# The S5 output maps of a hybrid decoder layer, made one step earlier in a generator

## The chip, the cores and the metric

The kernel runs on one core of a Trainium2 chip. The metric is the device time of one execution in microseconds; a time is the median of several executions. The core's engines are named as the profile names them: PE (matrix products; PEld are its weight loads), DVE (vector), ACT (scalar and activation functions), POOL (a second, general vector engine), SP (which here issues most DMAs). Each engine works through its own list of instructions in order and waits on semaphores for the others. SBUF is the on-chip memory that all engines read. PSUM is the accumulator memory that PE writes, divided here into eight banks of 512 float32 numbers per partition.

## The reference, cut to what matters

One decoder layer on a (1, 1024, 1024) float32 stream: a normalised input `h` is projected once by `w_in`, and the projection feeds three branches (an S5 state-space model, a Mamba-2 block and a cross-attention), which gates merge; then follow an output projection, a gated feed-forward block and a final norm. The change lies in the S5 branch:

```python
def s5_mixer(u, lam_re, lam_im, log_dt, b_re, b_im, c_re, c_im, d):
    ...
    bu_re = jnp.einsum('blgk,gpk->blgp', ug, bbr)
    bu_im = jnp.einsum('blgk,gpk->blgp', ug, bbi)
    ...
    _, _, xr, xi = lax.associative_scan(combine, (a_re, a_im, bu_re, bu_im), axis=1)
    y = jnp.einsum('gkp,blgp->blgk', c_re, xr) - jnp.einsum('gkp,blgp->blgk', c_im, xi)
    return y.reshape(bsz, L, D_S5) + d * u
```

There are 64 groups of 16 channels with 64 complex states each, over 1024 time steps.

## The kernel before, in words

**The stage.** The kernel computes the S5 recurrence in blocks of 8 time steps. The 64 groups are taken in four quarters (`q` = 0 to 3) of 16 groups. For one quarter it needs:

- *input maps* `BA` (`b_maps`, line 830): the matrices that carry 8 steps of input into one state, as products of `b` with powers of the state's multiplier. DVE makes them in six operations of 128x1024, all from SBUF to SBUF (`cmap`, line 816: four products, then a subtraction and an addition). PE transposes them in four blocks of four 128x128 pieces, each block into a PSUM bank `s5bps`, and ACT copies the blocks out as `s5BTr` and `s5BTi` (`b_transpose`, line 857).
- *output maps* `CA`: PE transposes the raw `c` into a PSUM bank `s5cps` (`c_transpose`, line 841, two matrix products); ACT copies that bank to the first step of `s5CAr` and `s5CAi`, and DVE makes the other eight steps with the same `cmap`, whose four products read `s5cps` from PSUM and whose last two operations read SBUF alone (`c_maps`, line 848).
- *lag matrices* (`lag_maps`, line 869): PE multiplies `CA` with `bd`, a block-diagonal copy of the input maps, into `s5kps` (16 pairs, `s5CAr` and `s5CAi` in turn). ACT copies the result, DVE adds the diagonal `s5dg`, and DMAs take it through the buffer `kS` in DRAM into `s5T`.
- *phases* `R`: POOL doubles the vectors `s5Rr` and `s5Ri` seven times (`double`, line 900).
- *sums, scan, back*: PE makes `s5sr` and `s5si` from the input and `BT`; DVE rotates them by `R`, scans, and rotates back into `s5Hr` and `s5Hi`.
- *outputs and gelu*, for the quarter before: PE makes `s5yp` from `s5T`, `s5Hr`, `s5Hi` and `CA`, in two halves `y0` and `y1`; ACT and DVE apply GELU to each half in turn (`gelu`, line 983), and DMAs store it.

**What runs beside it.** `s5_work` (line 778) is a generator. Between its `yield`s PE runs the matrix products of the projection: 4 query tiles `qt` and 9 gate tiles `gt`, each in two halves of 24 products 128x512 into a PSUM bank `gh`. After each 12 of them `tick` (line 329) is called, and lets the generator go on when its credit is positive; the numbers in `S5_LAG` (line 189) say how many ticks lie after each step. The weights of these tiles come by DMA into `wr`, and ACT and DVE split each into a high and a low part, `wh` and `wl`.

**What sets the order.** In this stage the order on PE, ACT and SP is that of the program text (`TE.on = SY.on = S.on = True`, line 1155). DVE and POOL are ordered by the scheduler of the tile framework, which also decides, by its own forecast of when buffers come free, which of the six small PSUM banks (pool `ps`) a tile gets. PE's waits follow from that choice.

**The names in the trace.** All instructions go through one helper, so that they all have line 51, and the tiles tell them apart. PE's products with 128x512 are written `gh<-hlH,wh` and so on.

Of the kernel before, what the change touches and what calls it, by code (L numbers as in the profile page):

```python
# [58 lines left out]
def hybrid_layer(ctx: ExitStack, tc: tile.TileContext, a: dict, out: bass.AP):  # L59
# [77 lines left out]
    def copy(o, i, scale=1.0):  # L137
        S.activation(out=o, in_=i, func=AF.Copy, scale=scale)
# [639 lines left out]
    def s5_work():  # L778

        with ExitStack() as es:  # L780
# [16 lines left out]
            def fl(t, s0, n):  # L797
                return t.rearrange("p j s k -> p j (s k)")[:, :, s0 * 16:(s0 + n) * 16]
# [17 lines left out]
            def cmap(o, s0, wr, wi, p2, jj):  # L816

                shp = [P, 8, 8, 16]
                orr, oi = (t[:, :, s0:s0 + 8, :] for t in o)
                w = [x.unsqueeze(2).to_broadcast(shp) for x in (wr, wi)]  # L820
                p_ = [bc(x[:, jj, :], 16) for x in p2]
                t1, t2 = (wt().rearrange("p j (t k) -> p j t k", t=8) for _ in range(2))
                tt(orr, w[0], p_[0], ALU.mult)
                tt(t1, w[1], p_[1], ALU.mult)
                tt(oi, w[0], p_[1], ALU.mult)
                tt(t2, w[1], p_[0], ALU.mult)
                tt(orr, orr, t1, ALU.subtract)
                tt(oi, oi, t2, ALU.add)

            def b_maps(jj, braw):  # L830

                BAr = sp.tile([P, 8, 8, 16], F32, tag="BAr", name="s5BAr")
                BAi = sp.tile([P, 8, 8, 16], F32, tag="BAi", name="s5BAi")
                cmap((BAr, BAi), 0, braw[:, 0], braw[:, 1], (pfr, pfi), jj)
                for g2 in range(2):
                    pp = slice(g2 * 64, (g2 + 1) * 64)
                    V.tensor_copy(bd[pp, 0, :, g2, :], BAr[pp, :, 7, :])
                    ts(bd[pp, 1, :, g2, :], BAi[pp, :, 7, :], -1.0, ALU.mult)
                return BAr, BAi

            def c_transpose(craw):
                cps = ps.tile([P, 2, 8, 16], F32, tag="s", name="s5cps")
                for ri in range(2):
                    TE.transpose(cps[:, ri].rearrange("p j k -> p (j k)"),
                                 craw[:, ri].rearrange("p g c -> p (g c)"), ident)
                return cps

            def c_maps(jj, cps):

                CAr = sp.tile([P, 8, 9, 16], F32, tag="CAr", name="s5CAr")  # L850
                CAi = sp.tile([P, 8, 9, 16], F32, tag="CAi", name="s5CAi")
                copy(CAr[:, :, 0, :], cps[:, 0])
                copy(CAi[:, :, 0, :], cps[:, 1])
                cmap((CAr, CAi), 1, cps[:, 0], cps[:, 1], (pwr, pwi), jj)
                return CAr, CAi
# [12 lines left out]

            def lag_maps(q, CA):

                ksq = kS[q % 2]
                ktw = wt()
                for hh in range(2):
                    kps = ps.tile([32, 4, P], F32, tag="s", name="s5kps")
                    for j in range(4):
                        jx = hh * 4 + j
                        for ri in range(2):
                            TE.matmul(kps[:, j, :], bd[:, ri, jx].rearrange("p g k -> p (g k)"),
                                      fl(CA[ri], 0, 8)[:, jx, :], start=ri == 0, stop=ri == 1)
                    KT = ktw[0:32, 4 * hh:4 * hh + 4, :]  # L880
                    copy(KT, kps)
                    dg = sp.tile([32, 4, 16], F32, tag="dg", name="s5dg")
                    tt(dg, bc(dk[:, 8 * q + 4 * hh:8 * q + 4 * hh + 4], 16),
                       id16.unsqueeze(1).to_broadcast([32, 4, 16]), ALU.mult)
                    tt(KT[:, :, 0:16], KT[:, :, 0:16], dg, ALU.add)
                    SY.dma_start(out=ksq[4 * hh:4 * hh + 4].rearrange("j p x -> p j x"), in_=KT)
                kv_ = ksq.rearrange("j (g k) x -> k j g x", g=2)
                for s in range(8):
                    tz = Tz[s * 16:(s + 1) * 16].rearrange("p (j g) t k -> p j g (t k)", g=2)
                    SY.dma_start(out=tz[:, :, :, s * 16:P], in_=kv_[:, :, :, 0:P - s * 16])  # L890

            def phases(jj):

                Rr = sp.tile([P, 8, P], F32, tag="Rr", name="s5Rr")
                Ri = sp.tile([P, 8, P], F32, tag="Ri", name="s5Ri")
                G.memset(Rr[:, :, 0:1], 1.0)
                G.memset(Ri[:, :, 0:1], 0.0)
                return Rr, Ri

            def double(R, jj, ks):  # L900
                Rr, Ri = R
                for k in ks:
                    n = 1 << k
                    tmp = sp.tile([P, 8, 64], F32, tag="ph", name="s5ph")[:, :, 0:n]
                    e_r, e_i = bc(er[:, k, jj], n), bc(ei[:, k, jj], n)
                    r0, i0, r1, i1 = Rr[:, :, 0:n], Ri[:, :, 0:n], Rr[:, :, n:2 * n], Ri[:, :, n:2 * n]
                    tt(r1, e_r, r0, ALU.mult, G)
                    tt(tmp, e_i, i0, ALU.mult, G)
                    tt(r1, r1, tmp, ALU.subtract, G)
                    tt(i1, e_r, i0, ALU.mult, G)  # L910
                    tt(tmp, e_i, r0, ALU.mult, G)
                    tt(i1, i1, tmp, ALU.add, G)
# [53 lines left out]

            def outputs(hh, U, CA):

                yps = [ps.tile([P, 4, P], F32, tag="s", name="s5yp") for _ in range(2)]
                for j in range(4):  # L970
                    jx = hh * 4 + j
                    for g2 in range(2):
                        g = 2 * jx + g2
                        TE.matmul(yps[g2][:, j, :], Tz[:, g].rearrange("p t k -> p (t k)"), U[:, g, :],
                                  start=True, stop=False)
                    for cm, hm, last in ((CA[0], Hr, False), (CA[1], Hi, True)):
                        for g2 in range(2):
                            pp = slice(g2 * 64, (g2 + 1) * 64)
                            TE.matmul(yps[g2][:, j, :], fl(cm, 1, 8)[pp, jx, :], hm[pp, jx, :],
                                      start=False, stop=last)  # L980
                return yps
# [23 lines left out]
            for q in range(5):  # L1005
                jj = slice(8 * q, 8 * q + 8)
                if old:
                    qo, Uo, CAo = old
                    y0 = outputs(0, Uo, CAo)
                if q < 4:  # L1010
                    U, braw, craw = nl
                    BA = b_maps(jj, braw)
                    R = phases(jj)
                    double(R, jj, range(5))
                yield S5_LAG[0]
                if old:
                    y1 = outputs(1, Uo, CAo)
                    Y0 = gelu(qo, 0, y0)
                if q < 4:
                    cps = c_transpose(craw)  # L1020
                    double(R, jj, [5])
                yield S5_LAG[1]
                if q < 4:
                    BT = b_transpose(BA)
                    double(R, jj, [6])
                    CA = c_maps(jj, cps)
                if old:
                    y_store(qo, 0, Y0)
                    Y1 = gelu(qo, 1, y1)
                yield S5_LAG[2]  # L1030
                if q == 4:
                    s5_end.append(lambda: y_store(qo, 1, Y1))
                    break
                lag_maps(q, CA)
                if old:
                    y_store(qo, 1, Y1)
                if q < 3:
                    nl = loads(q + 1)
                yield S5_LAG[3]
                D0 = decay(jj)  # L1040
                s0 = sums(0, BT, U)
                s1 = sums(1, BT, U)
                yield S5_LAG[4]
                W = [sp.tile([P, 8, P], F32, tag=t_, name="s5W") for t_ in ("BAr", "BAi")]
                scan(0, s0, R, D0, W)
                back(0, R, W)
                scan(1, s1, R, D0, W)
                yield S5_LAG[5]
                back(1, R, W)
                old = q, U, CA  # L1050

# [102 lines left out]
    set_banks("2", 1, 6, True)  # L1154
    TE.on = SY.on = S.on = True
    s5 = s5_work()
    next(s5)
    a1_epi(*a1_last[0])
# [298 lines left out]
    for m in G_SSD:  # L1457
        if m == G_SSD[-1]:
# [3 lines left out]
            cps = ExitStack()  # L1462
# [415 lines left out]
```

## Time and profile before

| | |
|---|---|
| time, median of 3 executions | 2279.96 us (2277.62 to 2281.93) |
| the profiled execution, its time | 2283.63 us |
| the profiled execution, its span (first to last instruction) | 2281.9 us |
| PE busy | 2212.3 us, 97% of the span |
| DVE busy | 1614.5 us, 71% |
| ACT busy | 988.3 us, 43% |
| POOL busy | 791.3 us, 35% |
| the stretch 515 to 754 us, in which the S5 stage lies | PE busy 225.88 of 239.00 us, DVE 186.48, ACT 65.58, POOL 118.38 |
| the stretch 754 to 906 us (attention) | PE busy 149.17 of 152.00 us |
| the stretch 1115 to 1532 us (merge) | PE busy 404.53 of 417.00 us |

A row of a timeline names the start, the duration, the engine and the operation, what it writes and reads, the sizes, and how many like it are merged; in brackets stands how long the engine had been idle before it, and what ended that. Matrix products are pipelined: the rows of PE overlap, and the distance between starts tells the rate. A row of waits says who waited for whom, microseconds in total, how often, and the longest. A row of windows gives a stretch, its length, the busy time of PE, PEld, DVE, ACT and POOL with their instruction counts, then the granted share of the PE clock, the share of the DMA engines and GB/s.

### The profile page before, as it was taken

The page shows a single profiled execution, that of the slowest core. Times are in us where ns is not written, and L with a number is a line of the kernel's source. Part 1 is how long each engine was busy: PE and PEld are TensorE (multiplying, and loading weights), DVE is VectorE, ACT ScalarE, POOL GpSimd, SP SyncE. Part 2 cuts the span into 40 slices and gives each one's busy share as a digit, 9 for nine tenths or more (in the row PEclk, how much of TensorE's full clock was granted, in tenths as well). Part 3 has the DMA queues.
Part 4 walks back from the last instruction along what each step waited for, and adds up shares of the span by engine and source line. Part 5 has one row for each costly group of instructions (what it writes and reads, how often), then busy time and mean ns, then how long its engine had stood idle before and what let it go on. Part 6 is the DMA issues. An engine that isn't in the chain of part 4 may idle for free. (4 is left out here: it accounts for less than half of the span.)

```text
span 2281.9 us, 31065 instructions
## 1 busy us (share of the span) xinstructions
PE 2212.3 (97%) x11243; PEld 1831.3 (80%) x11243; DVE 1614.5 (71%) x2354; ACT 988.3 (43%) x1750; POOL 791.3 (35%) x605
## 2 busy tenths in 40 slices
PE   7999899999999999999989999999999999999998
PEld 6887778887777887777768878889988888888886
DVE  7779966769777576989464445542898888886665
ACT  4555354552222466666242131222345555545544
POOL 2523333326554006888156512210023343320110
PEclk9999999999999999999999999999999999999999
DMA  4333233446454438888777664523323333339654
GB/s 142 120 109 105 84 111 111 148 134 138 78 114 100 142 117 268 300 293 270 248 248 233 219 216 128 166 67 119 111 79 102 106 101 108 99 102 330 220 184 163
DMA packets 380189, 355.53 MB, mean 156 GB/s; under 512 B 35586, under 2 KB 323202, under 8 KB 380036
## 3 DMA queue, kind: packets, MB, share of 16 engines
q1 hardware_dynamic: 378880, 349.36, 49.3%
q10 hardware_dynamic: 1156, 4.20, 0.5%
q8 instruction: 88, 1.44, 0.3%
q14 instruction: 65, 0.53, 0.1%
HBM read 255.45 MB, written 98.04 MB: 155 GB/s over the span
## 5 line engine op out<-in xcount | busy, mean ns | idle before, releaser
L51 DVE TENSOR_TENSOR wl<-wr,wh 128x512 fp32r<-128x512 f32 x301 | 257.5, 865 | 195.7 <-ACT wh L51 177.6
L51 ACT ACTIVATE wh<-wr 128x512 fp32r<-128x512 f32 (+1 forms) x305 | 186.7, 625 | 348.4 <-PE g L51 149.4
L51 POOL TENSOR_TENSOR wS<-wr 128x512 f32<-128x512 f32 x82 | 144.8, 1766 | 527.9 <-DMA wr<-in_w_up 330.5
L51 PE MATMUL g<-hlL,wh 128*128 128x512 f32 x736 | 290.0, 394 | 5.3 <-DVE hlL L51 5.3
L51 PE MATMUL g<-hlH,wh 128*128 128x512 f32 x736 | 288.8, 393 | 5.5 <-ACT hlH L51 4.4
L51 PE MATMUL g<-hlH,wl 128*128 128x512 f32 x736 | 288.0, 392 | 0.0
L51 PE MATMUL gh<-hlH,wh 128*128 128x512 f32 (+1 forms) x464 | 191.4, 413 | 0.0
L51 PE MATMUL gh<-hlH,wl 128*128 128x512 f32 (+1 forms) x464 | 181.4, 391 | 0.0
L51 PE MATMUL gh<-hlL,wh 128*128 128x512 f32 (+1 forms) x464 | 181.0, 390 | 0.0
L51 DVE TENSOR_TENSOR wl<-wS,wh 128x512 fp32r<-128x512 f32 x164 | 126.8, 778 | 65.9 <-ACT wh L51 65.9
L51 PEld LDWEIGHTS g<-hlL,wh 128*128 128x128 f32 x736 | 139.0, 189 | 38.8 <-DVE hlL L51 10.8
L51 PEld LDWEIGHTS g<-hlH,wh 128*128 128x128 f32 x736 | 139.0, 189 | 35.9 <-ACT hlH L51 5.7
L51 PEld LDWEIGHTS g<-hlH,wl 128*128 128x128 f32 x736 | 139.1, 189 | 28.4
L51 ACT ACTIVATE wh<-wS 128x512 fp32r<-128x512 f32 x164 | 102.9, 628 | 127.3 <-PE wA L51 69.3
L51 POOL TENSOR_TENSOR wS<-wr,wS 128x512 f32<-128x512 f32 x41 | 93.9, 2289 | 121.0 <-DVE wl L51 119.7
L51 PE MATMUL dP<-wl,ah 128*128 128x512 f32 x308 | 120.1, 390 | 0.4 <-DVE wl L51 0.4
L51 PE MATMUL dP<-wh,ah 128*128 128x512 f32 x308 | 120.0, 389 | 0.1
L51 PE MATMUL dP<-wh,al 128*128 128x512 f32 x308 | 119.8, 389 | 0.0
L51 PEld LDWEIGHTS gh<-hlH,wh 128*128 128x128 f32 (+1 forms) x464 | 85.9, 185 | 23.9 <-issue 5.6
L51 DVE TENSOR_TENSOR al<-ra,ah 128x512 fp32r<-128x512 f32 x77 | 56.2, 730 | 67.0 <-ACT ah L51 66.9
L51 PEld LDWEIGHTS gh<-hlL,wh 128*128 128x128 f32 (+1 forms) x464 | 86.0, 185 | 21.5 <-issue 3.6
L51 PEld LDWEIGHTS gh<-hlH,wl 128*128 128x128 f32 (+1 forms) x464 | 85.8, 185 | 20.3
(382 smaller groups left out, 5822.7 us busy)
## 6 DMA issues: line engine op xcount, KB each, us to landing
wr<-in_w_in SPq DMA_DIRECT2D x76, 512.0 KB, 3.7
wr<-in_w_up SPq DMA_DIRECT2D x44, 512.0 KB, 3.7
xc<-xcS SPq DMA_DIRECT2D x32, 640.0 KB, 6.0
ra<-aS SPq DMA_DIRECT2D x77, 256.0 KB, 5.0
seg<-aD SPq DMA_DIRECT2D x32, 512.0 KB, 7.4
gi<-gS SPq DMA_DIRECT2D x32, 512.0 KB, 5.1
xcS<-xv SPq DMA_DIRECT2D x24, 512.0 KB, 2.9
gS<-gt SPq DMA_DIRECT2D x24, 512.0 KB, 3.8
```

Of the source, the lines that this page charges most:

```text
L51: r = f(*args, **kw)
```

## The change

The call of `c_maps` moves from behind `b_transpose`, one `yield` later, to directly behind `c_transpose`.

```diff
@@ -1017,13 +1017,12 @@
                     y1 = outputs(1, Uo, CAo)
                     Y0 = gelu(qo, 0, y0)
                 if q < 4:
-                    cps = c_transpose(craw)
+                    CA = c_maps(jj, c_transpose(craw))
                     double(R, jj, [5])
                 yield S5_LAG[1]
                 if q < 4:
                     BT = b_transpose(BA)
                     double(R, jj, [6])
-                    CA = c_maps(jj, cps)
                 if old:
                     y_store(qo, 0, Y0)
                     Y1 = gelu(qo, 1, y1)
```

No instruction is added or dropped. The order on SP, on POOL and of PE's matrix products stays as it was; what moves stands on ACT, on DVE in quarter 0 alone, and in the PSUM banks, and so in PE's waits.

ACT, quarter 1 (`s5Y` is the GELU of half `y0`, `qt<-gh` copies out a query tile, `s5BTr` and `s5BTi` copy out the four transposed blocks of the input maps; the words in brackets are the counters that a row waits for):

```order
 L51 ACTIVATE s5Y<-s5yp 128x4x128 [waits PE_49]
 L51 ACTIVATE s5Y<-s5Y 128x4x128 [waits DVE_49]
-L51 ACTIVATE qt<-gh 128x512 [waits PE_49,Activation_49,Pool_49]
+L51 ACTIVATE s5CAr<-s5cps 128x8x16 [waits PE_49]
+L51 ACTIVATE s5CAi<-s5cps 128x8x16
+L51 ACTIVATE qt<-gh 128x512 [waits Activation_49,Pool_49]
 L51 ACTIVATE s5BTr<-s5bps 128x512 [waits PE_49] x2
 L51 ACTIVATE s5BTi<-s5bps 128x512 [waits PE_49] x2
-L51 ACTIVATE s5CAr<-s5cps 128x8x16
-L51 ACTIVATE s5CAi<-s5cps 128x8x16
```

The two copies out of `s5cps` now stand ahead of the four copies of `s5bps`, and ahead of the copy of a projection tile. In the other quarters it is the same, but in quarter 0 they stand behind `qt<-gh`.

PE, quarter 1, the third and fourth block of the transposition of the input maps:

```order
 L51 MATMUL s5bps<-ident,s5BAi 128x128 [waits DVE_49,PE_49]
 L51 MATMUL s5bps<-ident,s5BAi 128x128 x3
-L51 MATMUL s5bps<-ident,s5BAi 128x128 [waits Activation_49]
+L51 MATMUL s5bps<-ident,s5BAi 128x128 [waits DVE_49,PE_49,Activation_49]
 L51 MATMUL s5bps<-ident,s5BAi 128x128 x3
```

The fourth block used to take the bank of the first one, once ACT had copied that out. Now it takes the bank of `s5cps`, and its first product waits for the fourth DVE product of the output maps, the last reader of that bank. Quarter 3 has the same new wait; in quarter 2 the fourth block keeps the bank of the first and its wait for ACT, and in quarter 0 it has no wait.

DVE, quarter 0, from the block-diagonal copies `s5bd` to the output maps:

```order
 L51 COPY s5bd<-s5BAr 64x8x16
 L51 TENSOR_SCALAR s5bd<-s5BAi 64x8x16
-L51 TENSOR_TENSOR s5dg<-s5dk,id_395 32x64
 L51 TENSOR_TENSOR s5CAr<-s5cps,s5pwr 128x8x128
 L51 TENSOR_TENSOR s5w<-s5cps,s5pwi 128x1024
```

The small diagonal `s5dg` goes from ahead of the output maps to behind them and the two `wl` that follow them. In quarters 1 to 3 DVE's order is unchanged: the output maps already stood directly behind the GELU of half `y0`.

## The prediction

> **What bounds the kernel now.** PE does: it is busy for 97% of the span. So I read first what PE waits for in the S5 stretch (waits, 515 to 760 us: who waited for whom, microseconds in total, times, longest).
>
> ```profile
> DVE s5CAr L51 <- ACT s5CAi L51: 18.3, 4, 7.0
> ...
> PE s5kps L51 <- DVE s5CAr L51: 6.9, 4, 1.9
> PE s5kps L51 <- DVE s5CAi L51: 6.2, 4, 1.8
> ```
>
> PE has no other wait there: 13.1 us in eight pieces, all at the lag matrices `s5kps`, all for DVE's last two operations of the output maps. DVE in turn had been idle for 18.3 us ahead of those maps, waiting for ACT's copy `s5CAi`. The timelines of the three engines in quarter 1 show why.
>
> ```profile
> 579.80 0.44 PE L51 MATMUL s5cps<-ident,s5bc 128*128 128x128 f32 x2
> 585.56 1.03 PE L51 MATMUL s5bps<-ident,s5BAr 128*128 128x128 f32 x8
> 586.43 1.07 PE L51 MATMUL s5bps<-ident,s5BAi 128*128 128x128 f32 x8
> 594.61 0.38 PE L51 MATMUL s5kps<-s5CAr,s5bd 128*32 128x128 f32 x2 [1.64 <-DVE s5CAr L51]
> 596.59 0.38 PE L51 MATMUL s5kps<-s5CAi,s5bd 128*32 128x128 f32 x2 [1.60 <-DVE s5CAi L51]
> ...
> 580.33 0.63 ACT L51 ACTIVATE s5Y<-s5Y 128x512 f32<-128x512 f32 x1 [0.86 <-DVE s5Y L51]
> ...
> 586.20 1.09 ACT L51 ACTIVATE s5BTr<-s5bps 128x512 f32<-128x512 f32 x2 [4.75 <-PE s5bps L51]
> ...
> 588.28 0.32 ACT L51 ACTIVATE s5CAi<-s5cps 128x128 f32<-128x128 f32 x1
> ...
> 581.00 0.69 DVE L51 SCALAR_TENSOR_TENSOR s5Y<-s5Y,s5yp 128x512 f32<-128x512 f32 x1 [0.70 <-ACT s5Y L51]
> 588.63 1.23 DVE L51 TENSOR_TENSOR s5CAr<-s5cps,s5pwr 128x1024 f32<-128x1024 f32 x1 [6.95 <-ACT s5CAi L51]
> ...
> 592.04 1.21 DVE L51 TENSOR_TENSOR s5w<-s5cps,s5pwr 128x1024 f32<-128x1024 f32 x1
> ...
> 594.38 2.06 DVE L51 TENSOR_TENSOR s5CAi<-s5CAi,s5w 128x1024 f32<-128x1024 f32 x1
> ```
>
> PE has transposed `c` by 580.24, but ACT copies it at 588.28, behind the copies of `s5bps`, which PE makes only at 585.56. DVE, free at 581.69, starts 6.95 us later and ends at 596.44; PE, ready for `s5kps` at 592.97 (594.61 less 1.64), stalls.
>
> The stall costs more than its length. The windows (length, busy of PE, PEld, DVE, ACT, POOL, then the granted PE clock) show PE at half clock behind it, in all four quarters:
>
> ```profile
> 539.00:543.00 4.00, 4.00 (x24) 3.43 (x23) 2.85 (x3) 0.59 (x1) 3.92 (x4) 0.57 0.13 25
> 597.00:600.50 3.50, 3.50 (x19) 2.85 (x18) 2.01 (x4) 2.56 (x5) 0.62 (x2) 0.51 0.02 5
> 600.50:604.00 3.50, 3.50 (x55) 3.29 (x55) 2.46 (x7) 3.18 (x6) 0.00 (x0) 1.00 0.56 171
> 651.50:655.00 3.50, 3.50 (x19) 2.92 (x20) 2.11 (x4) 2.22 (x5) 3.27 (x4) 0.53 0.00 0
> 710.00:713.00 3.00, 3.00 (x16) 2.49 (x15) 1.61 (x4) 1.96 (x4) 1.78 (x3) 0.50 0.00 0
> ```
>
> Length times the missing share is 1.72, 1.72, 1.65 and 1.50 us; I take 1.7 each, 6.8 in all.
>
> **The change part by part.** Nothing is added or removed; ACT's two copies and DVE's six operations start earlier. The sum is made in the profiled execution (2283.63 us, span 2281.9).
>
> *Quarter 0.* Here DVE has little idle time to give:
>
> ```profile
> 529.40 0.22 DVE L51 TENSOR_SCALAR s5bd<-s5BAi 64x128 f32<-64x128 f32 x1
> 529.63 0.21 DVE L51 TENSOR_TENSOR s5dg<-s5dk,id 32x64 f32<-32x64 f32 x1
> 531.01 1.22 DVE L51 TENSOR_TENSOR s5CAr<-s5cps,s5pwr 128x1024 f32<-128x1024 f32 x1 [1.17 <-ACT s5CAi L51]
> ...
> 537.25 0.38 PE L51 MATMUL s5kps<-s5CAr,s5bd 128*32 128x128 f32 x2 [1.81 <-DVE s5CAr L51]
> 538.80 0.38 PE L51 MATMUL s5kps<-s5CAi,s5bd 128*32 128x128 f32 x2 [1.17 <-DVE s5CAi L51]
> ...
> 545.57 1.29 POOL L51 TENSOR_TENSOR s5Ri<-s5Ri,s5ph 128x512 f32<-128x512 f32 x1
> ...
> 548.85 0.69 DVE L51 TENSOR_TENSOR s5w<-s5si,s5Ri 128x512 f32<-128x512 f32 x1 [0.17 <-PE s5si L51]
> ```
>
> The maps start at 529.62, when `s5bd` is done, not 531.01: 1.39 us earlier. Of PE's 2.98 us, 1.59 remain. Does the clock still drop? Two other gaps bound that:
>
> ```profile
> 812.00:816.00 4.00, 3.32 (x16) 2.72 (x17) 3.70 (x11) 3.29 (x11) 0.00 (x0) 1.00 0.08 30
> 1334.50:1337.50 3.00, 3.00 (x11) 2.46 (x10) 2.42 (x6) 0.00 (x0) 0.00 (x0) 0.50 0.44 131
> ...
> 812.68 0.59 PE L51 MATMUL ptps<-ident,pr 128*128 128x128 f32 x2 [2.12 <-DVE pr L51]
> ...
> 1333.12 0.60 PE L51 MATMUL ib<-dgi,ones 128*128 128x128 f32 x3 [1.86 <-DVE dgi L51]
> ```
>
> A gap of 2.12 us kept the full clock, one of 1.86 lost it; 1.59, in two pieces, lies below both, so I take no drop and keep 1.7 us for the range. Quarter 0 gains 1.39 + 1.7 = 3.1. The moved `s5dg` (0.21 us) falls into DVE's wait for `s5kps` and costs nothing, at most 0.2.
>
> *Quarter 1.* From `s5kps` on, DVE's scan follows PE's sums, so DVE moves with PE, with one exception: POOL's phases end at 546.86 whatever PE does, and DVE needs them at 548.85. DVE can come at most 1.9 us earlier while PE comes 3.1. The maps then start at 581.69 - 1.9 = 579.8, right behind `s5Y`, and their fourth product ends 4.62 us later (588.63 to 593.25), at 584.4. The maps are whole 3.2 us after that (593.25 to 596.44), at 587.6, and PE reaches `s5kps` at 589.9 at the earliest: the wait of 3.24 us and its half clock go. The new wait takes some back: the fourth transposed block stood at 586.87 (586.43 and four steps of 0.11) and is due at 586.87 - 3.1 = 583.8, 0.65 us before its bank is free. Behind it in PE's list stand the projection products of two ticks and then `s5kps`, and for the block itself wait ACT's last copy to `s5BTi` and, queued behind that on ACT, the GELU of half `y1`; all of these have the 5 us and more until `s5kps`, so the price is PE's own 0.65. Net 3.24 + 1.7 - 0.65 = 4.3. Lower bound of the new wait: 0, if POOL doesn't hold DVE back; upper: 1.2 more if DVE gains nothing in quarter 0.
>
> *Quarter 2* has no new wait at the fourth block.
>
> ```profile
> 638.08 0.69 DVE L51 SCALAR_TENSOR_TENSOR s5Y<-s5Y,s5yp 128x512 f32<-128x512 f32 x1 [0.70 <-ACT s5Y L51]
> ...
> 649.45 0.38 PE L51 MATMUL s5kps<-s5CAr,s5bd 128*32 128x128 f32 x2 [1.59 <-DVE s5CAr L51]
> ```
>
> DVE is free at 638.77; with the 7.8 us that the six operations took in quarter 1 (588.63 to 596.44) the maps are whole at 646.6, and PE comes to `s5kps` at 647.86. That is enough by 1.3 us, the smallest margin of the three. The old wait is 13.1 less the 2.98, 3.24 and 3.71 of the others, so 3.2 with rounding, and 1.7 of clock: 4.9.
>
> *Quarter 3:*
>
> ```profile
> 695.12 0.69 DVE L51 SCALAR_TENSOR_TENSOR s5Y<-s5Y,s5yp 128x512 f32<-128x512 f32 x1 [0.70 <-ACT s5Y L51]
> ...
> 699.07 1.07 PE L51 MATMUL s5bps<-ident,s5BAi 128*128 128x128 f32 x8
> 707.49 0.38 PE L51 MATMUL s5kps<-s5CAr,s5bd 128*32 128x128 f32 x2 [1.88 <-DVE s5CAr L51]
> 709.69 0.58 PE L51 MATMUL s5kps<-s5CAi,s5bd 128*32 128x128 f32 x2 [1.83 <-DVE s5CAi L51]
> ```
>
> DVE starts the maps at 695.81, their fourth product ends at 700.43, and the fourth block stood at 699.51: PE waits 0.9. Gain 3.71 + 1.7 - 0.9 = 4.5.
>
> ACT's copies (0.3 us each) take ACT's idle time, 4.75 us in quarter 1; what they delay is one copy of a projection tile, whose bank PE needs ticks later: 0, at most 0.3 a quarter.
>
> No DMA is moved: SP's list is the same, its stores and loads wait for results of DVE and ACT that come earlier or keep their place against PE, and PE waits for no DMA in this stretch. Past the stage PE's list is unchanged, and what it saved moves everything behind it forward as a block.
>
> Sum: 3.1 + 4.3 + 4.9 + 4.5 = **16.8 us**. The profiled execution would take 2266.8. It was 3.7 us above the median of the runs, so the median goes from 2279.96 to **2263.2**.
>
> [...]
>
> **The rivals.**
>
> *The half clock stays.* It may belong to the narrow `s5kps` products, on which all four slow stretches lie, and not to the gaps. Against: within the same run of products it is back at 1.00 at 600.5, and it came behind other products at 1334.5. Then 16.8 - 6.8 = 10.0: 2270.0. [...] Chance 0.08.
>
> *The new wait takes the old one's place.* If DVE comes to the maps 1.4 us later against PE than computed, the fourth block waits 2 us in quarters 1 and 3 and the clock drops behind it: 3.7 each where I have 0.65 and 0.9, 5.9 us less: 2269.1. For it: DVE has no slack there. Against: in quarter 3 the relation is read directly. Chance 0.08.
>
> *The gain is lost later* (the change does nothing for the end). The chain of waits of the merge stage goes through DMAs; if these kept their own time, PE would wait there. Against: its first long piece is PE's own, and the DMAs come behind it;
>
> ```profile
> 1183.81 3.49 PE g L51 x14
> ```
>
> what PE does earlier there lets those transfers go earlier. Time 2280. Chance 0.06.
>
> *Slower.* The earlier maps run beside more of POOL's phases; if POOL holds each of the four products as it held small operations of DVE in quarter 0,
>
> ```profile
> 545.60 1.34 DVE L51 TENSOR_TENSOR s5dg<-s5dk,id 32x64 f32<-32x64 f32 x1
> ...
> 588.27 1.05 POOL L51 TENSOR_TENSOR s5Rr<-s5keep,s5Rr 128x512 f32<-128x512 f32 x1
> ```
>
> 1.34 for 0.21, that is 1.13 each, 4.5 by the fourth product. Against the kernel before, quarter 0 then loses 4.5 - 1.4 = 3.1; quarter 1 waits 3.9 at the fourth block and 1.7 of clock for its 4.9, loses 0.7; quarter 2 stands even; quarter 3 has 0.9 + 4.5 + 1.7 for 5.4, loses 1.7: 5.5 slower, 2285.5. It decides from about 0.8 per product. Against: the four products ran 1.14 us apart from 588.63 to 592.04 with POOL working beside them, as the last row shows. Chance 0.04.
>
> **How the numbers follow.** The forecast has 0.74. Its own ends: 2260.0 if no wait is left at all (13.1 + 6.8 = 19.9), 2265 if quarter 0 keeps its half clock; the first two rivals go to 2270.0, and the runs of before spread by 4.3 us, 2 to each side. So 2257 to 2273. A measurement of this kernel tells about 0.2% (4.6 us) from no change: faster 0.74 + 0.08 + 0.08 = 0.90, same 0.06, slower 0.04.
>
> **What would show it.** In the changed profile: PE's waits for `s5CAr` and `s5CAi` only in quarter 0, some 1.6 us; DVE's idle time ahead of `s5CAr` under 0.3 us in quarters 1 to 3; new PE waits at `s5bps` for DVE's `s5w`, under 1 us, in quarters 1 and 3 and not in 2; a clock of 1.00 from 515 to 740; and PE's later stages the same length, begun 17 us earlier. I am wrong if PE waits over 1.9 us at `s5bps`, if the clock falls without a gap, or if the stages from 754 us on grow.

## The result, and the profile after

The changed kernel takes 2266.92 us, the median of four executions (2265.27 to 2269.32), against 2279.97 us (2277.62 to 2281.93) for the kernel before, run beside it. The ratio is 0.9945, with a 95% interval of 0.9932 to 0.9957: 13 us faster, where 16.8 were forecast (2263.2 us, with a range of 2257 to 2273). The profiled execution took 2266.93 us with a span of 2265.2.

The waits of the changed kernel from 500 to 750 us (who waited for whom, microseconds in total, times, longest):

```profile
DVE s5w L51 <- POOL s5Ri L51: 1.2, 1, 1.2
...
PE s5kps L51 <- DVE s5CAi L51: 1.2, 1, 1.2
...
PE s5bps L51 <- ACT s5BTi L51: 0.8, 1, 0.8
...
PE s5kps L51 <- DVE s5CAr L51: 0.5, 1, 0.5
```

Of eight waits at the lag matrices, two are left, both in quarter 0. DVE's 18.3 us of waiting for ACT ahead of the maps are gone. One new wait of 0.8 us has come, at the transposed input maps `s5bps`. DVE now begins the maps of quarter 1 right behind its GELU operation (timeline of DVE, quarters 0 and 1):

```profile
529.33 1.22 DVE L51 TENSOR_TENSOR s5CAr<-s5cps,s5pwr 128x1024 f32<-128x1024 f32 x1
...
546.70 0.69 DVE L51 TENSOR_TENSOR s5w<-s5si,s5Ri 128x512 f32<-128x512 f32 x1 [1.25 <-POOL s5Ri L51]
...
578.31 0.69 DVE L51 SCALAR_TENSOR_TENSOR s5Y<-s5Y,s5yp 128x512 f32<-128x512 f32 x1 [0.70 <-ACT s5Y L51]
578.92 1.22 DVE L51 TENSOR_TENSOR s5CAr<-s5cps,s5pwr 128x1024 f32<-128x1024 f32 x1
...
582.31 1.21 DVE L51 TENSOR_TENSOR s5w<-s5cps,s5pwr 128x1024 f32<-128x1024 f32 x1
...
584.67 1.63 DVE L51 TENSOR_TENSOR s5CAi<-s5CAi,s5w 128x1024 f32<-128x1024 f32 x1
```

The windows (length, busy time of the five engines, granted PE clock, DMA share, GB/s) have the full clock where the kernel before had half of it, and half clock at one new place, in the attention stage:

```profile
539.00:543.00 4.00, 4.00 (x26) 3.40 (x24) 3.76 (x5) 2.57 (x4) 3.92 (x5) 1.00 0.59 147
...
592.00:595.50 3.50, 3.50 (x53) 3.30 (x53) 3.50 (x4) 2.25 (x4) 3.34 (x3) 1.00 0.21 47
637.00:642.00 5.00, 5.00 (x36) 4.30 (x35) 3.29 (x6) 2.85 (x6) 4.84 (x6) 1.00 0.00 0
691.00:695.00 4.00, 4.00 (x28) 3.38 (x27) 2.98 (x4) 2.57 (x5) 3.92 (x5) 1.00 0.19 80
...
795.00:798.00 3.00, 3.00 (x10) 2.52 (x10) 2.93 (x8) 2.25 (x9) 0.00 (x0) 0.50 0.00 0
```

Where the time went is read from PE's first product of each stage. After:

```profile
524.55 0.38 PE L51 MATMUL s5cps<-ident,s5bc 128*128 128x128 f32 x2
...
535.69 0.38 PE L51 MATMUL s5kps<-s5CAr,s5bd 128*32 128x128 f32 x2 [0.55 <-DVE s5CAr L51]
537.25 0.38 PE L51 MATMUL s5kps<-s5CAi,s5bd 128*32 128x128 f32 x2 [1.18 <-DVE s5CAi L51]
...
687.04 0.63 PE L51 MATMUL s5bps<-ident,s5BAi 128*128 128x128 f32 x4 [0.80 <-ACT s5BTi L51]
...
794.64 1.16 PE L51 MATMUL ptps<-ident,pr 128*128 128x128 f32 x4 [2.12 <-DVE pr L51]
...
871.33 0.47 PE L51 MATMUL yo<-xc,Hs 128*128 128x128 f32 x2
...
1515.72 0.28 PE L51 MATMUL wops<-wh,hlH 128*128 128x256 f32 x1
```

Before (the first `ptps` stands in the prediction, at 812.68):

```profile
524.85 0.38 PE L51 MATMUL s5cps<-ident,s5bc 128*128 128x128 f32 x2
...
887.94 1.14 PE L51 MATMUL yo<-xc,Hs 128*128 128x128 f32 x8
...
1532.43 0.28 PE L51 MATMUL wops<-wh,hlH 128*128 128x256 f32 x1
```

I call the stretch from the first `s5cps` to the first `ptps` the *front*; it holds all that the change touches. It took 287.83 us before and takes 270.09 us now: 17.7 less. From `ptps` to `yo` (attention) it was 75.26 and is 76.69: 1.4 more. From `yo` to `wops` (state space and merge) it was 644.50 and is 644.39. So these two profiled executions differ by 16.7 us: 17.7 of the front less the 1.4 of the attention stage, plus 0.1, plus 0.3 by which the changed kernel's trace had reached its first `s5cps` sooner (524.55 against 524.85). That this is nearly the 16.8 of the forecast is in part chance. The medians differ by 13.

### The profile page after: what moved, and what is told of

It reads as the page before. It is cut to its first block, busy times and chain, and to the rows that moved or that the text cites. A ratio compares the mean times of both kernels' runs of the same rounds, so it can differ in the third digit from the quotient of the medians.

```text
span 2265.2 us, 31065 instructions
## 1 busy us (share of the span) xinstructions
PE 2205.7 (97%) x11243; PEld 1828.4 (81%) x11243; DVE 1620.4 (72%) x2354; ACT 987.8 (44%) x1750; POOL 795.9 (35%) x605
## 5 line engine op out<-in xcount | busy, mean ns | idle before, releaser
L51 DVE TENSOR_TENSOR wl<-wr,wh 128x512 fp32r<-128x512 f32 x301 | 262.5, 882 | 198.4 <-ACT wh L51 194.7
```

The costliest lines, as they stand in the source:

```text
L51: r = f(*args, **kw)
```

## The experiments

Each run left one trace; the kernel before has three. The ratios are against executions of the kernel before that were run beside each kernel. Front, attention and the stretch from `yo` to `wops` are read from each as above:

| kernel | time, median us | ratio to before (95%) | front | attention | `yo` to `wops` |
|---|---|---|---|---|---|
| before, first trace | 2279.97 | | 287.83 | 75.26 | 644.50 |
| before_look_1, before_look_2 | 2281.99, 2278.80 (one each) | | 287.73, 287.62 | 76.91, 75.25 | 640.49, 639.47 |
| the change | 2266.92 | 0.9945 (0.9932 to 0.9957) | 270.09 | 76.69 | 644.39 |
| copies_early | 2267.34 | 0.9939 (0.9927 to 0.9952) | 270.06 | 76.67 | 643.76 |
| filled_gaps | 2273.43 | 0.9970 (0.9958 to 0.9981) | 281.80 | 76.84 | 640.87 |
| from_quarter_1 | 2267.86 | 0.9950 (0.9931 to 0.9969) | 272.80 | 76.81 | 643.78 |
| one_tick_more_q0 | 2266.02 | 0.9947 (0.9934 to 0.9960) | 273.31 | 76.76 | 638.94 |
| product_doubled | 2265.19 | 0.9934 (0.9921 to 0.9948) | 271.93 | 76.89 | 645.70 |
| maps_before_copies | 2263.97 | 0.9925 (0.9908 to 0.9941) | 269.12 | 76.85 | 638.48 |
| before_spread | 2281.14 | 1.0005 (0.9996 to 1.0014) | 287.28 | 75.25 | 641.81 |
| after_spread | 2263.73 | 0.9926 (0.9912 to 0.9940) | 270.14 | 75.25 | 644.79 |
| all_three | 2264.32 | 0.9931 (0.9918 to 0.9943) | front and attention 344.38 | | 642.64 |
| maps_first_filled | 2260.04 | 0.9910 (0.9892 to 0.9929) | front and attention 343.93 | | 638.91 |

The front of one program repeats within 0.2 us (before_spread, whose edit lies behind the front, has 0.3 to 0.6 less than the three traces of before); the stretch from `yo` to `wops` doesn't. So the steps of the prediction are tested on the front, and the rest by itself.

### What DVE waited for: copies_early and maps_before_copies

```diff
                     cps = c_transpose(craw)
+                    CA = c_copies(cps)
...
-                    CA = c_maps(jj, cps)
+                    cmap(CA, 1, cps[:, 0], cps[:, 1], (pwr, pwi), jj)
```

`c_copies` holds ACT's two copies alone.

> Only ACT's two copies of the transposed c stand at the earlier place; the call of DVE's six operations stands where it did before. Theory (DVE waited for nothing but ACT's place in its own list): the whole gain, 13 to 16.7 us below the kernel before (2263 to 2267 us), DVE's map operations begin at 578.9 us in quarter 1 as with the full change, and PE waits 1.7 us at s5kps in quarter 0 alone. Rival (DVE's operations had to be moved in the text as well): the eight PE waits of 13.1 us stay and the time is 2280.

The scheduler put DVE's operations where the change has them, and the instruction lists of all engines are those of the change. The front is 270.06 us against 270.09. So it was enough to move ACT's two copies in ACT's list; where the call of DVE's six operations stands in the text is of no account. The run is at the same time a second sample of the changed program's times.

```diff
+                cmap((CAr, CAi), 1, cps[:, 0], cps[:, 1], (pwr, pwi), jj)
                 copy(CAr[:, :, 0, :], cps[:, 0])
                 copy(CAi[:, :, 0, :], cps[:, 1])
-                cmap((CAr, CAi), 1, cps[:, 0], cps[:, 1], (pwr, pwi), jj)
```

> The kernel before with one exchange: at the old place, behind the evacuation of the transposed input maps, DVE's six operations are called first and ACT's two copies behind them. No transposition and no copy is made earlier. Theory (DVE waited for nothing but ACT's copies into the same tile): DVE begins the maps as early as with the change (578.9 us in quarter 1), in quarters 1 to 3 PE doesn't wait at s5kps; in quarter 0 the copies, 0.6 us, now lie behind the maps and PE waits 2.3 us, which may or may not cost 1.7 us of clock: 347.4 to 349.1 us from the first s5cps to the first yo, against 363.1 before and 346.8 with the change. Rival (DVE has to wait for something else at the old place, the bank or its own list): 361 to 363, no gain.

From the first `s5cps` to the first `yo` it took 269.12 + 76.85 = 345.97 us, less than either theory gave, and 0.8 less than the change. DVE begins the maps of quarter 1 at 578.89 us, as with the change. The waits of this kernel, and quarter 3 on PE and DVE:

```profile
ACT s5CAr L51 <- DVE s5w L51: 3.6, 1, 3.6
```

```profile
685.61 1.07 PE L51 MATMUL s5bps<-ident,s5BAi 128*128 128x128 f32 x8
685.66 1.22 DVE L51 TENSOR_TENSOR s5w<-s5cps,s5pwr 128x1024 f32<-128x1024 f32 x1
```

Two things follow. The copies now wait for DVE's fourth product (`s5w`), not for the whole maps, so the 0.6 us that I had charged to quarter 0 isn't paid. And in quarter 3 the eight steps of the third and fourth block run on without a wait, though the fourth product ends at 686.88, as late as with the change (where `s5w` began at 685.68), and though ACT's copy `s5BTi` comes as it did there. So the new wait of 0.80 us wasn't for ACT's copy, as its row names it, and the product's end by itself isn't its cause either. It is the bank: with the change the scheduler gives the fourth block of quarters 1 and 3 the bank of `s5cps`, which DVE reads until its fourth product; here, as in the kernel before, it gives it the bank of the first block. The instructions show it: in these two the first product of the fourth block waits for ACT's counter alone, with the change for DVE's and PE's as well.

That DVE and ACT are kept in the order of the text although both only read `s5cps` and write separate slices of `s5CAr` and `s5CAi` is shown both ways round. Whether the framework does it for the bank or for the tile that both write stays open.

### The half clock: filled_gaps

```diff
                     kps = ps.tile([32, 4, P], F32, tag="s", name="s5kps")
+                    for i in range(4 if hh == 0 else 0):
+                        TE.matmul(kps, ident[:, 0:32], U[:, 4 * i:4 * i + 4, :], start=True, stop=True)
```

> The kernel before, with four added products of 512 columns (0.88 us each by the 0.22 us of an s5kps product of 128 columns, 3.5 us together) in PE's list ahead of the first s5kps of each quarter. They need nothing from the output maps and are overwritten. DVE and ACT stay as late as before. Theory (the half clock comes from the gaps): the waits of 2.98, 3.24, 3.2 and 3.7 us are filled but not gained, the products stand over them by some 1 us in all, and the clock stays at 1.00 behind them: 4 x 1.7 - 1 = 5.8 us faster, 2274. Rival (the half clock belongs to the narrow s5kps products or to a calendar of its own): still 0.50 behind them, no gain, 2280 to 2281.

PE's list in quarter 0, and the windows behind the four fills:

```profile
534.60 3.62 PE L51 MATMUL s5kps<-s5U,ident 128*32 128x512 f32 x8
538.06 0.38 PE L51 MATMUL s5kps<-s5CAr,s5bd 128*32 128x128 f32 x2
538.28 0.38 PE L51 MATMUL s5kps<-s5CAi,s5bd 128*32 128x128 f32 x2
```

```profile
539.00:543.00 4.00, 4.00 (x31) 3.58 (x30) 3.69 (x5) 1.83 (x4) 3.92 (x4) 1.00 0.33 73
...
595.00:599.00 4.00, 4.00 (x48) 3.80 (x48) 2.48 (x4) 3.13 (x7) 0.40 (x2) 1.00 0.07 28
...
650.00:654.00 4.00, 4.00 (x24) 3.04 (x23) 3.20 (x4) 3.70 (x7) 3.05 (x4) 1.00 0.32 131
...
706.00:710.00 4.00, 4.00 (x57) 3.80 (x56) 2.99 (x6) 3.13 (x7) 0.73 (x2) 1.00 0.27 104
```

DVE is as late as before, PE does 3.5 us of useless work in each quarter, and the front is 281.80 us: 5.9 shorter than the mean of the three traces of before (287.73), where 5.8 was expected. The narrow products run at full clock (1.00 in all four windows). The half clock came from the gaps, and its four pieces are worth the 6.8 us of the sum.

### The quarters by themselves: from_quarter_1 and one_tick_more_q0

```diff
-                    CA = c_maps(jj, c_transpose(craw))
+                    cps = c_transpose(craw)
+                    CA = c_maps(jj, cps) if q else None
...
                     double(R, jj, [6])
+                    CA = CA or c_maps(jj, cps)
```

> The change in quarters 1 to 3 alone; quarter 0 as before. Theory (the quarters add up): quarter 0 gives back its 2.9 us, the others keep 5.1, 5.1 and 4.6: 349.7 us from the first s5cps to the first yo. Rival (the later quarters lived on what quarter 0 had gained, or quarter 0's loss gives DVE room in quarter 1 that shows later): more than 1 us off that, either way.

272.80 + 76.81 = 349.61 us. The quarters add up, and the later ones don't live on quarter 0.

```diff
-                yield S5_LAG[2]
+                yield S5_LAG[2] + (1 if q == 0 else 0)
```

> The change, with one more group of 12 projection products (2.8 us) ahead of the lag matrices of quarter 0 alone. Theory: PE's last wait at s5kps (1.73 us in quarter 0) goes, the later quarters keep theirs, 1.7 us below the change: 15 to 18 us below the kernel before. Rival: DVE's scan of quarter 0 comes later by the group, so DVE is later for the maps of quarter 1 and the fourth transposed block waits there for its bank (1 us or more): no gain over the change.

Against the change the front is 3.2 us longer, not 1.7 shorter. PE's waits in quarter 0 are gone, but in quarter 1 two new ones stand, 2.0 us at `s5sr` and 0.9 at `s5si`, with half clock behind them (timeline and window):

```profile
598.08 1.09 PE L51 MATMUL s5sr<-s5U,s5BTr 128*64 128x128 f32 x16 [2.00 <-DVE s5Y L51]
```

```profile
600.10:603.50 3.40, 3.40 (x20) 2.78 (x21) 1.73 (x6) 1.55 (x3) 0.00 (x0) 0.50 0.15 39
```

So the theory falls and the rival is right in kind, though at another bank than it named: PE waits at the sums for DVE's GELU operation. The median of 2266.0 us doesn't show the loss: in the trace (2265.65 us) the stretch from `yo` to `wops` was among the shortest, and two of the five executions took 2272.5.

### The bank of the fourth block: product_doubled

```diff
+                if s0:
+                    tt(orr, w[0], p_[0], ALU.mult)
                 tt(orr, w[0], p_[0], ALU.mult)
```

> The change, with the first of DVE's four map products made twice, so that the fourth product ends 1.14 us later in each quarter. Theory (at the fourth transposed block PE waits for DVE's fourth product): 1.1 us more at s5kps in quarter 0, about 1.0 us of new wait at s5bps in quarter 1 where there was none, nothing in quarter 2 (1.8 us of room at s5kps), 1.1 more than the 0.80 in quarter 3; where a wait passes 1.9 us the half clock returns for 1.7 us. Sum 3.2 us slower than the change, 4.9 with one half clock. Rival (the wait in quarter 3 is for ACT's copy to s5BTi, as the row of the profile names it): quarter 1 stays without a wait and quarter 3 keeps 0.80: 1.1 us slower than the change.

Quarter 0 lost 2.8 us against the change, as much as the theory's 1.1 of wait and 1.7 of clock. (That the half clock returns beyond 1.9 us was my estimate; no run shows it as a bound.) But in quarters 1 and 3 there is no wait at `s5bps`, so that quarter 3 gained 0.95 and the front is 1.8 us longer: less than the 3.2 or 4.9 of the theory and more than the 1.1 of the rival, so neither is borne out. Quarter 1 on DVE and PE:

```profile
585.91 1.21 DVE L51 TENSOR_TENSOR s5w<-s5cps,s5pwr 128x1024 f32<-128x1024 f32 x1
...
586.08 1.07 PE L51 MATMUL s5bps<-ident,s5BAi 128*128 128x128 f32 x8
```

In quarter 1 the blocks go through while the fourth product still runs. In this program the scheduler gave the fourth block of both quarters the bank of the first block, not that of `s5cps` (its first product waits for ACT's counter alone). So this run doesn't tell how the wait grows with DVE's lateness, which it was meant to; that stays untested. It shows, as maps_before_copies does, that the wait hangs on the choice of the bank.

### Where 4 us of the gain went: before_look, before_spread, after_spread

> The kernel before, unchanged, for another trace. In the first one PE took 363.1 us from the first s5cps to the first yo, with the half clock behind all four pairs of gaps, and 644.5 us from there to the first wops. Theory A (the stage is fixed, the spread of the times sits in the merge stage): 363.1 to 363.3, or 364.5 to 364.8 if the gap of 2.12 us in the attention stage loses the clock as in the trace after; four half clocks at s5kps; and 639 to 646 from yo to wops. [...]

> [...]

Both traces have the same eight waits and four half clocks at `s5kps` (the granted clock is 0.50 behind each), and fronts of 287.73 and 287.62 us. The waits of before_look_1, and its windows at the gap of 2.12 us in the attention stage (810.65 to 812.78 there):

```profile
DVE s5CAr L51 <- ACT s5CAi L51: 18.4, 4, 6.9
...
PE s5kps L51 <- DVE s5CAr L51: 6.8, 4, 1.9
PE s5kps L51 <- DVE s5CAi L51: 6.2, 4, 1.8
```

```profile
809.20:812.60 3.40, 1.45 (x13) 1.25 (x11) 2.78 (x9) 1.49 (x5) 0.00 (x0) 1.00 0.98 371
812.60:816.00 3.40, 3.22 (x10) 2.66 (x11) 3.16 (x10) 2.83 (x10) 0.00 (x0) 0.50 0.02 7
```

Theory A holds: the front is fixed, and the spread lies behind it. The attention stage is some 1.5 us longer in some executions than in others (76.67 to 76.91 us against 75.25 and 75.26), and `yo` to `wops` took between 638.5 and 645.7 us over all traces. If the front of its trace is taken from each time, 47 executions of the kernel before leave a median of 1992.7 us for the rest, and the 9 executions of the changed program (the change and copies_early) leave 1996.8. These 4 us separate 17.7 from 13 to 14. They are uncertain by about 2 us, and they don't come with every shorter front: the five other kernels that shorten it and leave the later stages alone (filled_gaps, from_quarter_1, one_tick_more_q0, product_doubled and maps_before_copies, 24 executions) have median rests of 1991.6 to 1995.1.

Nearly all that varies between `yo` and `wops` is PE's waits and the clock: less PE's idle time, and less half of the time at half clock, this stretch is 619.1 to 621.0 us long in all 14 traces (644.49 less 18.36 of idle time and 5.12 of clock in the first trace of before, 644.39 less 18.44 and 6.84 in the change's). One wait of the merge stage shows it. The changed kernel, on PE (with the window behind it), DVE, ACT and SP's queue:

```profile
1316.63 1.03 PE L51 MATMUL ib<-dgi,ones 128*128 128x128 f32 x4 [3.08 <-DVE dgi L51]
...
1316.90:1320.30 3.40, 3.40 (x13) 3.01 (x13) 2.86 (x6) 0.60 (x1) 0.00 (x0) 0.50 0.68 223
```

```profile
1314.56 0.69 DVE L51 TENSOR_TENSOR wl<-wr,wh 128x512 fp32r<-128x512 f32 x1 [5.71 <-ACT wh L51]
```

```profile
1313.89 1.15 ACT L51 ACTIVATE wh<-wr 128x512 fp32r<-128x512 f32 x2 [9.63 <-DMA wr<-in_w_b]
```

```profile
1308.23 0.46 SPq L51 DMA_DIRECT2D wr<-in_w_b  x1
```

The kernel before in the trace before_look_2, PE, ACT and SP:

```profile
1329.26 0.71 PE L51 MATMUL ib<-dgi,ones 128*128 128x128 f32 x4 [1.01 <-DVE dgi L51]
```

```profile
1326.52 1.16 ACT L51 ACTIVATE wh<-wr 128x512 fp32r<-128x512 f32 x2 [9.31 <-PE g L51]
```

```profile
1321.14 0.45 SPq L51 DMA_DIRECT2D wr<-in_w_b  x1
```

Eleven traces have the merge stage as it was (all but before_spread, after_spread and all_three). Five of them (the first trace of before, the change, copies_early, from_quarter_1 and product_doubled) have 643.8 to 645.7 us from `yo` to `wops`; the six others have 638.5 to 640.9. So the long form of this stage goes with this wait (1.9 to 4.3 us in the five, at most 1.8 in the six), and in the two of the five whose clock stands here also with a half clock behind it (0.50 from 1334.50 to 1337.50 us in the first trace of before, from 1316.90 to 1320.30 in the change's; 1.7 us each).

DVE's `dgi` stands behind its share of a weight split, that behind ACT's `wh`, and that, with the change, behind a load that SP issues 8.4 us (1316.63 less 1308.23) ahead of the product in the one and 8.1 in the other; counted from PE's arrival (1313.55 and 1328.25) it is 5.3 against 7.1. In before_look_2 the row of `wh` names PE's `g` and not the load: by this row the load had come in time there. Ahead of that load SP's list has the loads and stores of the generator `down_sums`, which wait for POOL and for each other's transfers. To test this chain I thinned it:

```diff
         og = gemm_fm(("p", "w_a_gate", 0, KD, m * P, P), mv_c(cg), m == 0)
         next(yn, None)
-        next(dn, None)
```

> The kernel before, with one call taken out of the merge stage: the generator down_sums (POOL's sums of the down weights with their loads and stores on SP's queue) is advanced once for each of the 8 tile pairs of the first loop instead of twice, so that its 22 steps reach into the second loop. Nothing is left out and the S5 stage is untouched. In ten traces PE took 638.5 to 645.7 us from the first yo to the first wops, and the four longest had its longest wait (2.8 to 4.3 us for dgi) behind a weight load that stands in SP's list behind these loads and stores. Theory (that chain makes the spread): the wait for dgi falls under 1 us, yo to wops 635 to 640, the time 2274 to 2279 with a spread of less than 5 us. Rival (the spread comes from elsewhere, or the chain only moves): 639 to 646 as before, or a new wait in the second loop.

> The change, with the same call taken out of the merge stage. Theory (the change loses 3 to 4 us of its 16 in the merge stage by way of that chain): yo to wops within 1.5 us of the one of before with the same edit, and the times of the two differ by 15.5 to 18 us instead of 13.3, so 2257 to 2263. Rival (the later stages lose it in another way): the difference stays at 12 to 14 us, and yo to wops is 2 to 5 us longer than in before with the same edit.

The waits of after_spread from 1096 to 1513 us:

```profile
PE g L51 <- ACT sg L51: 2.4, 1, 2.4
PE ib L51 <- DVE dgi L51: 1.4, 3, 0.9
```

The single long wait for `dgi` is gone from both kernels, but another (for `sg`, 2.4 and 2.2 us) takes its place (longer waits for `hlH`, 4.3 and 3.9 us, stand in these two traces as in the others), and `yo` to `wops` is 641.8 and 644.8 us, not 635 to 640: the edit saves nothing by itself (before_spread has a ratio of 1.0005). With it the rests are alike: medians of 1993.9 us (11 executions) and 1993.6 (5). The two times differ by 17.4 us, within the theory's 15.5 to 18 and near the 17.1 of the fronts (287.28 less 270.14). The two traces by themselves go the rival's way: `yo` to `wops` is 3.0 us longer with the change, where the theory allowed 1.5. By the medians, the changed front is worth its 17 us in the time when the merge stage's chain is arranged in another way. By the intervals 17.4 isn't far from 13 to 14 (each ratio is uncertain by about 3 us), so I call it probable, not shown, that the plain pair loses its 4 us there: about 1 in the attention stage (76.67 us or more in 1 of 3 traces before, in 2 of 2 after), the rest in the merge stage (643.8 us or more from `yo` to `wops`, again in 1 of 3 and in 2 of 2, which at some 5 us each is about 3). Three traces and two are few for this. Why the changed program meets the long form of that stage more often stays open.

### Versions that go further: all_three and maps_first_filled

```diff
             tp_ = ps.tile([P, 2, 2, P], F32, tag="s", name="ptps")
+            for _ in range(fill):
+                TE.matmul(tp_[:, 0, 0, :], ident, ident, start=True, stop=True)
```

`fill` is 9 for the first unit of the attention stage and 0 for all others.

> Three edits together: the six map operations called ahead of the two copies at the old place, the thinner calls of down_sums, and 9 products of 128 columns (0.22 us each by the s5kps products, 2.0 us) in PE's gap of 2.12 us at the first ptps of the attention stage, which need nothing and are overwritten. Theory (a filled gap keeps the clock): ptps to yo 75.3 us instead of 76.8, no half clock there; s5cps to ptps 269.1 as with the exchange alone; with the merge stage as in the run of the change with that edit the time is 2.4 us below it (1.0 of the stage, 1.4 of the clock). Rival (the half clock in the attention stage isn't due to that gap): 76.8 us and half clock as before.

Front and attention together took 344.38 us, 1.6 less than with the exchange alone (345.97). The thinner `down_sums` brought nothing to it: 2264.32 us, where 2.4 less than the 2263.73 of after_spread were expected.

> The exchange (map operations ahead of the copies at the old place) with the 9 filling products in the attention stage's gap, and the merge stage as in the kernel before. Theory: the stage and the fill add up in the trace, 344.4 us from the first s5cps to the first yo (346.8 with the change, 363.1 before), no half clock in the attention stage; the merge stage comes out anywhere between 638.5 and 645.7 us as in the other traces, so the median lies between 2259 and 2266. Rival (what the front gains is taken back behind it in full): yo to wops over 646 us and the time no lower than the change's 2267.

PE at the first `ptps`, and the window behind it:

```profile
792.11 2.17 PE L51 MATMUL ptps<-ident 128*128 128x128 f32 x18
794.39 0.81 PE L51 MATMUL ptps<-ident,pr 128*128 128x128 f32 x4
```

```profile
793.00:798.00 5.00, 4.89 (x30) 4.08 (x29) 4.18 (x13) 4.03 (x15) 0.00 (x0) 1.00 0.20 82
```

The gap is filled, the clock behind it is 1.00, and front and attention take 343.93 us (344.4 expected). The time is 2260.04 us, ratio 0.9910 (0.9892 to 0.9929): 20 us below the kernel before, and below the change.

## Why the prediction was right or wrong

*What bounds the kernel, and what DVE waited for.* Right. PE's eight waits came from DVE's late maps, these from ACT's copies, and these from their place in ACT's list: moving the copies alone gives all of it, and so does calling the maps ahead of them.

*The clock term, 1.7 us in each quarter.* Right. Filling the gaps without making DVE faster gave 5.9 us, where 6.8 less about 1 for the overhang was expected. The rival that the half clock stays with the narrow products falls: with the gaps filled they ran at 1.00. No gap of this stage is longer than 1.9 us in the kernel before, and the half clock came all four times. That quarter 0 keeps the full clock came true (1.00 from 539 to 543 us, behind waits of 0.55 and 1.18), but by luck: a gap of 2.12 us that kept the clock and one of 1.86 that lost it give no bound for the length of a gap, and the gap of 2.12 us at the same place lost the clock in before_look_1 and in the change's trace (0.50 in both). How near quarter 0 came to losing it is not shown.

*The quarters.* PE's first products of the next step show what each gained:

| quarter | forecast | measured | why |
|---|---|---|---|
| 0 | 3.1 | 2.9 | 1.73 us of wait remain, not 1.59; no half clock, as said |
| 1 | 4.3 | 5.1 | the new wait of 0.65 us did not come |
| 2 | 4.9 | 5.1 | |
| 3 | 4.5 | 4.6 | the new wait was 0.80, not 0.9 |
| sum | 16.8 | 17.7 | |

The mis-sized term is the new wait of quarter 1. I let DVE come 1.9 us earlier, held by POOL's phases. That part was right: measured from the first `s5cps` of each trace (524.85 and 524.55), DVE's operation behind POOL (548.85 before, 546.70 after, with 1.25 us of idle time) came 1.85 us earlier. What I left out is 0.44 us of DVE's waiting for ACT behind the scan, which fell away as well. In the kernel before it stood here:

```profile
554.62 1.29 DVE L51 TENSOR_TENSOR wl<-wr,wh 128x512 fp32r<-128x512 f32 x2 [0.44 <-ACT wh L51]
```

So `s5Y` ended 2.4 us earlier on that scale (581.69 and 579.00), and PE came 2.9 us earlier and not 3.1. The fourth product then ended at 583.52 and the block was due at 583.65: no wait, with 0.13 us to spare. That the fourth block shares the bank of `s5cps` in quarters 1 and 3 and not in 2 was right; the row of the profile that names ACT for it is not.

*From the front to the end.* Here a step failed: "what it saved moves everything behind it forward as a block". Between the two profiled executions it nearly held (1.4 us given back in the attention stage, 16.7 in all). Over the executions on record the rest became about 4 us longer (uncertain by about 2), so the median fell by 13 to 14 us. That a stage from 754 us on grows was one of the signs of being wrong that the prediction named: the attention stage did, by 1.4 us with its half clock, and by the medians the stages behind it did too. Where exactly the 4 us go is not shown. The rival that the gain is lost later had the right stage, but it is part of the gain and not all of it.

*The step to the median.* I took the 3.7 us by which the profiled execution stood above the median along into the forecast. This excess lay in the merge stage (644.50 us there, 640.49 and 639.47 in the two other traces), which each execution draws anew; it says nothing of the next kernel. As it happened, 2263.2 is what the typical rest of before and the new front give (1992.7 + 270.1 = 2262.8), and the measured 2266.9 differs from it by the 4 us named above.

*The slower rival.* POOL didn't stretch the four products: they start 1.13 us apart from 578.92 to 582.31, as before.

## What to carry to other kernels

Ask of every wait which list the late instruction stands in, and whether its place there is needed: two copies of 0.3 us, queued behind work that they didn't depend on, cost 17 us of this front. Price a PE gap with the clock that it costs behind it (1.5 to 1.7 us behind each pair of gaps here), and where the gap can't be removed, products without use may fill it (5.9 us of the front in filled_gaps). Read the gain of an edit on the stretch that it touches, over more than one trace, and don't carry the surplus of one execution, or the full gain, through a later stage that has its own chain of transfers.

## What the runs showed of the hardware

PE's gaps, as its rows name them, and the clock granted behind them, as the windows have it:

| trace | where | gaps, us | granted clock behind (window, us) |
|---|---|---|---|
| before, first trace | `s5kps`, quarter 0 | 1.81 and 1.17 | 0.57 (539.00 to 543.00) |
| | `s5kps`, quarter 1 | 1.64 and 1.60 | 0.51 (597.00 to 600.50) |
| | `s5kps`, quarter 2 | 1.59 and 1.60 | 0.53 (651.50 to 655.00) |
| | `s5kps`, quarter 3 | 1.88 and 1.83 | 0.50 (710.00 to 713.00) |
| | `ptps` | 2.12 | 1.00 (812.00 to 816.00) |
| | `ib` | 1.86 | 0.50 (1334.50 to 1337.50) |
| before_look_1 | `ptps` | 2.12 | 0.50 (812.60 to 816.00) |
| the change | `s5kps`, quarter 0 | 0.55 and 1.18 | 1.00 (539.00 to 543.00) |
| | `ptps` | 2.12 | 0.50 (795.00 to 798.00) |
| | `ib` | 3.08 | 0.50 (1316.90 to 1320.30) |
| one_tick_more_q0 | `s5sr` and `s5si`, quarter 1 | 2.0 and 0.9 | 0.50 (600.10 to 603.50) |
| filled_gaps | `s5kps`, quarter 0 | filled | 1.00 (539.00 to 543.00) |
| maps_first_filled | `ptps` | filled | 1.00 (793.00 to 798.00) |

In the kernel before, the half clock came behind four pairs of gaps of 1.17 to 1.88 us and behind a single gap of 1.86. The gap of 2.12 us at `ptps` was followed by full clock in one trace of the kernel before and by half clock in another. So in these traces the length of a gap doesn't tell by itself whether the clock falls; what does is not shown. Where it fell behind that gap, the attention stage was 1.4 to 1.7 us longer (76.69 us in the change's trace and 76.91 in before_look_1, against 75.26).
